# Gated unit ahead of the attention, late gates and key projections between the read-outs, mixing in each attention step, output projection by sequences

## The chip, the cores and the metric

The kernel runs on one core of one Trainium2 chip. The metric is the device time of one execution in microseconds. Five engines work side by side, each through its own list of instructions in order: TensorE (PE; its weight loads are listed apart as PEld), VectorE (DVE), ScalarE (ACT), GpSimd (POOL) and SyncE (SP). Most transfers are issued from SP's list, some from ACT's and POOL's, and an engine goes on once it has issued one.

## The reference, cut to what matters

One encoder layer is applied to two sequences of 512 tokens, width 1024, all in float32:

```python
h = rms_norm(x, ln1)
q, k, v, u, g_att, g_ssm = jnp.split(h @ w_in, IN_SPLITS, axis=-1)
q = rms_norm(q.reshape(..., 16, 64), q_gain); k = rms_norm(k.reshape(..., 4, 64), k_gain)
y_att = windowed_attention(q, k, v, sink, bias, band_mask(seq_len))
y = gelu(s5(u))
y_ssm = y * sigmoid(y @ w_glu + b_glu)
mixed = sigmoid(g_att) * y_att + sigmoid(g_ssm) * y_ssm
x = x + mixed @ w_out
h2 = rms_norm(x, ln2)
return x + square(relu(h2 @ w_up)) @ w_down
```

`s5` is a state-space recurrence in both directions over 64 groups of 16 channels. The attention has 16 heads in 4 groups (j), a band of 128 to each side and blocks of 128 queries.

## The kernel before, in words

Every large product is made in three passes (`mm3`, L164 to L166): each operand is split into a rounded part (hi, cast on ACT) and a rest (lo, subtracted on DVE), and PE adds hi·hi, lo·hi and hi·lo in one bank. So every weight that comes in passes ACT and then DVE before PE can use it.

The stages, by the times of the profile:

- 0 to 228: norm of the input, the columns of u, tables for the recurrence.
- 212 to 394: sixteen gate columns (`gate_column`; L187 evacuates, L188 writes to `ga_scr` and `gs_scr`), while DVE runs the recurrence over 64 chunks (233 to 348).
- 394 to 480: four row tiles of keys, then the states are read out. One q stands for two groups: `st` is copied from the states (L477, L479, L480), PE multiplies it with the tables `toep` (L484) and `ctab` (L487) that SP loads (L464, L466, L471), ACT applies gelu (L489), and each eight groups go out in one write from ACT's queue (L493).
- 480 to 538: the other keys in turn with four query tiles, then the values.
- 538 to 775: the attention, eight steps (j, sequence) of four units. PE, ACT and DVE follow an order written out by hand here; POOL and SP are ordered by a scheduler. A unit makes the scores of one query block, and in between projects one query tile for the next step: its norm runs over POOL (L623, L624: power; L629: copy `qn`) before PE turns it (L634). `Divide` takes the sums of a finished step, turns them, writes them out and reads them back spread over the partitions (`fac`, L724 to L730), and POOL multiplies the step's result with them (L735), which goes to `mix_scr` (L736). During step 7 the state branch's y, turned in memory by eight copies, is read back and split (L901, L902).
- 775 to 893: the gated unit, for sequence 1 and then 0, eight columns each: weights (L138, L139), gates and attention's result loaded, sigmoids (L918, L919), products on POOL (L922, L923), PE, sigmoid (L926), product and sum (L927, L928), split (L929, L930).
- 893 to 1000: output projection, row tile by row tile (both sequences' tile t in turn), each followed by norm and turning (L980, L985).
- 1000 to 1629: the MLP's two products by a scheme of seven block products; the change doesn't touch them.

Each engine's instructions outside the part ordered by hand stand in the order that the scheduler gave them. A pool's buffers decide when a load may start: it waits until the last reader of the buffer is done.

## Time and profile before

| | us |
|---|---|
| three runs | 1626.48, 1618.11, 1625.65 |
| median | 1625.65 |
| profiled execution, span | 1629.0 |
| PE busy | 1522.8 (93%) |
| DVE busy | 1140.7 (70%) |
| ACT busy | 794.0 (49%) |
| POOL busy | 172.7 (11%) |
| mean granted clock of PE | 0.977 |

The span is the time from the first to the last instruction of one execution. Matmuls overlap, so the sum of their busy time says less than the distance from start to start. A wait in the list of waits is put down to what came last.

### The profile page before, as it was taken

What the parts mean: (1) busy time and instruction counts of PE and PEld (TensorE: products, weight loads), DVE (VectorE), ACT (ScalarE), POOL (GpSimd) and SP (SyncE); (2) the same over time, 40 slices, a digit from 0 to 9 for tenths busy, and PEclk for the clock granted to TensorE, in tenths of its full rate; (3) what the DMA queues carried; (4) which work ended last, traced back from release to release, by engine and by line L of the source; (5) the groups of instructions that cost most, each with busy time, mean ns of one, the idle gap of its engine ahead of it and who ended that gap; (6) DMA issues with size and microseconds to landing.
All of it is one profiled execution on the core that took longest, in us unless ns stands there. A gap on an engine that the chain in (4) does not pass through costs nothing.

```text
span 1629.0 us, 22424 instructions
## 1 busy us (share of the span) xinstructions
PE 1522.8 (93%) x8202; PEld 1293.8 (79%) x8202; DVE 1140.7 (70%) x2006; ACT 794.0 (49%) x1398; POOL 172.7 (11%) x246
## 2 busy tenths in 40 slices
PE   4999999999779999998688997999999999999999
PEld 3778878888669988995467997888888878888787
DVE  7899969961434788889778546777777659666544
ACT  5667751222332678779555323445545434433332
POOL 2000001000013123332452000000000000000000
PEclk9999999999879999999899998999999999999999
DMA  4444458233863132213575422544444397445331
GB/s 158 131 147 142 144 172 279 98 110 111 278 211 107 33 96 76 84 55 105 199 237 171 154 84 95 168 143 142 149 149 158 131 351 258 143 145 177 124 122 65
DMA packets 115226, 240.24 MB, mean 147 GB/s; under 512 B 15355, under 2 KB 38011, under 8 KB 115116
## 3 DMA queue, kind: packets, MB, share of 16 engines
q1 hardware_dynamic: 93100, 191.47, 36.6%
q10 hardware_dynamic: 19456, 37.87, 6.1%
q0 software_dynamic: 2560, 9.48, 1.7%
q8 instruction: 64, 1.05, 0.3%
q14 instruction: 46, 0.38, 0.1%
HBM read 169.53 MB, written 81.82 MB: 154 GB/s over the span
## 4 chain that ended last, share of the span: by engine, by line
PE 72%; DVE 8%; DMA 7%; issue 6%; ACT 4%; POOL 2%; SPq 0%; ACTq 0%; POOLq 0%; DVEq 0%
PE bank L165 12%; PE bank L166 12%; PE bank L164 12%; PE acc L165 7%; PE acc L166 7%; PE acc L164 7%; PE acc L611 4%; DMA ctab_in<-ct_scr 3%; PE sps L389 2%; PE sps L409 2%; PE sps L487 2%; PE po L696 1%; DMA k<-in_w_down_dram 1%; PE sps L664 1%; PE tps L680 1%
## 5 line engine op out<-in xcount | busy, mean ns | idle before, releaser
L165 PE MATMUL bank<-b_lo,a_hi 128*128 128x512 f32 x448 | 175.2, 391 | 3.3 <-DVE b_lo L1125 3.3
L166 PE MATMUL bank<-b_hi,a_lo 128*128 128x512 f32 x448 | 175.0, 391 | 0.0
L164 PE MATMUL bank<-b_hi,a_hi 128*128 128x512 f32 x448 | 174.2, 391 | 0.0
L164 PE MATMUL acc<-hT,c_hi 128*128 128x512 f32 x384 | 152.6, 397 | 0.0
L165 PE MATMUL acc<-hT,c_hi 128*128 128x512 f32 x384 | 152.5, 397 | 0.0
L166 PE MATMUL acc<-hT,c_lo 128*128 128x512 f32 x384 | 151.1, 393 | 0.0
L164 PE MATMUL bank<-act,u_hi 128*128 128x512 f32 x376 | 147.6, 393 | 3.3 <-ACT u_hi L1022 3.3
L1124 ACT CAST a_hi<-d_a 128x1024 fp32r<-128x1024 f32 x56 | 59.0, 1054 | 182.3 <-PE bank L165 178.4
L165 PE MATMUL bank<-act,u_hi 128*128 128x512 f32 x376 | 147.5, 392 | 0.0
L166 PE MATMUL bank<-act,u_lo 128*128 128x512 f32 x376 | 146.9, 391 | 0.0
L1125 DVE TENSOR_TENSOR a_lo<-d_a,a_hi 128x1024 fp32r<-128x1024 f32 x56 | 68.5, 1223 | 99.7 <-ACT a_hi L1124 97.7
L611 PE MATMUL acc<-w_hi,hT 128*128 128x256 f32 x512 | 116.1, 295 | 0.0
L165 PEld LDWEIGHTS bank<-b_lo,a_hi 128*128 128x128 f32 x448 | 84.5, 189 | 22.1 <-DVE b_lo L1125 4.4
L166 PEld LDWEIGHTS bank<-b_hi,a_lo 128*128 128x128 f32 x448 | 84.4, 188 | 17.6
L164 PEld LDWEIGHTS bank<-b_hi,a_hi 128*128 128x128 f32 x448 | 84.5, 189 | 17.5
L139 DVE TENSOR_TENSOR c_lo<-c_raw,c_hi 128x512 fp32r<-128x512 f32 x80 | 60.9, 765 | 43.1 <-ACT c_hi L138 42.9
L611 PEld LDWEIGHTS acc<-w_hi,hT 128*128 128x128 f32 x512 | 87.0, 189 | 3.8
L138 ACT CAST c_hi<-c_raw 128x512 fp32r<-128x512 f32 x80 | 49.1, 618 | 83.5 <-PE acc L165 47.5
L164 PEld LDWEIGHTS bank<-act,u_hi 128*128 128x128 f32 x376 | 71.2, 189 | 18.7 <-ACT u_hi L1022 3.7
L164 PEld LDWEIGHTS acc<-hT,c_hi 128*128 128x128 f32 x384 | 72.7, 189 | 15.6 <-issue 1.5
L165 PEld LDWEIGHTS acc<-hT,c_hi 128*128 128x128 f32 x384 | 72.7, 189 | 15.2 <-issue 1.1
L166 PEld LDWEIGHTS acc<-hT,c_lo 128*128 128x128 f32 x384 | 72.5, 189 | 14.8 <-issue 0.2
(292 smaller groups left out, 3899.8 us busy)
## 6 DMA issues: line engine op xcount, KB each, us to landing
d_a<-a_scr SPq DMA_DIRECT2D x56, 512.0 KB
u_raw<-in_w_up_dram SPq DMA_DIRECT2D x32, 512.0 KB
a_scr<-t ACTq DMA_DIRECT2D x64, 256.0 KB
k<-in_w_down_dram SPq DMA_DIRECT2D x32, 512.0 KB
c_raw<-in_w_ug_dram SPq DMA_DIRECT2D x48, 256.0 KB
a_scr<-a ACTq DMA_DIRECT2D x48, 256.0 KB
ct_scr<-ctab SPq DMA_DIRECT2D x16, 576.0 KB
ctab_in<-ct_scr SPq DMA_DIRECT2D x16, 576.0 KB
```

Of the source, the lines that this page charges most:

```text
L138: S.copy(hi[:, sl, :], raw)
L139: sub(lo[:, sl, :], raw, hi[:, sl, :].bitcast(F32))
L164: PE.matmul(ps, a[0], b[0], start=first, stop=False)
L165: PE.matmul(ps, a[0], b[1], start=False, stop=False)
L166: PE.matmul(ps, a[1], b[0], start=False, stop=last)
L389: PE.matmul(ps[0:48, g * 144:(g + 1) * 144], lbt[:, ri, q * SG + gp * SH + g, :], ctab[:, gp * SH + g, ri].rearrange("p n c -> p (n c)"), ...
L409: PE.matmul(ps[:, i * P:(i + 1) * P], bm[:, ri, g, :], u_sb[:, gp * SH + g, :], start=True, stop=True)
L487: PE.matmul(o, ctab[:, g0 % SI + g, ri, 0:T * CH], st[:, ri, g].rearrange("p s k -> p (s k)"), start=False, stop=ri == 1)
L611: PE.matmul(self.ps, hT[sq][act][:, k, col:col + P], w[:, k % 4, :], start=i == 0, stop=i == 3 * KT - 1)
L664: PE.matmul(ps[:, 0:self.nk], qs, kk[:, self.k0 * P:self.k1 * P], start=i == 0, stop=i == 1)
L1124: S.copy(hi, src)
L1125: V.tensor_sub(lo, src, hi.bitcast(F32))
```

## The change

The change moves whole stages.

- Gates: `Gate` loads, multiplies and evacuates in pieces. Thirteen columns are made whole as before; the last three (`LATE`) and all eight row tiles of keys become a list `work` that is dealt out between the 32 read-outs. The gate of the attention gets its sigmoid at the evacuation, and that of the state branch is written in the order of y.
- Read-out: PE, ACT and DVE follow an order by hand. Tables come per two q (four groups). Each two q's result leaves in eight writes of 16 partitions from SP (L587), in the order in which y is read back later, so the eight copies in memory are gone.
- Values and y: during the eight row tiles of values y is read and split.
- The gated unit stands ahead of the attention; each column's weights are loaded once for both sequences, and the result, with its gate, goes to `z_scr`.
- Entry: the four query tiles of the first step follow one another.
- Attention: `Divide.multiply` multiplies with the factor (L903) and with the attention's gate (L905) and adds z (L906), on POOL. In step 7 the mixed rows of steps 0 to 5 are read back and split (L921 to L924); those of steps 6 and 7 are split from their buffers (`parts`, L915, L916).
- Output projection: sequence 0 by blocks of 256 columns, its rows kept in `x1p`, then sequence 1 by row tiles.

In the code `V` is DVE, `S` ACT, `GP` POOL, `SP` SyncE.

```diff
+LATE = 3
...
-    y_scr = dram.tile([T, CH, GROUPS, NSEQ * NCHUNK], F32, name="y_scr")
-    y2_scr = dram.tile([GROUPS, CH, T, NSEQ * NCHUNK], F32, name="y2_scr")
+    y_scr = dram.tile([GROUPS, CH, T, NSEQ * NCHUNK], F32, name="y_scr")
...
+    class Gate:
...
+        def evacuate(self, s):
+            if s == 0:
+                self.sg = evp.tile([P, NTOK], F32, tag="ev", name="sg")
+            if self.kind == "ga":
+                S.activation(self.sg[:, s * HALF:(s + 1) * HALF], self.ps[s], AF.Sigmoid)
+            else:
+                S.copy(self.sg.rearrange("p (t s k) -> p t s k", t=T, s=NSEQ)[:, :, s, :],
+                       self.ps[s].rearrange("p (k t) -> p t k", t=T))
+            if s == 1:
+                SP.dma_start((ga_scr if self.kind == "ga" else gs_scr)[self.c], self.sg)
...
-        gates = [(scr, base, c) for scr, base in ((ga_scr, GA_BLK), (gs_scr, GS_BLK)) for c in range(KT)]
-        for i, (scr, base, c) in enumerate(gates[:10]):
-            gate_column(c, scr, base)
+        gates = [Gate(c, kind) for kind in ("ga", "gs") for c in range(KT)]
+        for i, gate in enumerate(gates[:-LATE]):
+            gate.whole()
...
-                if (g0 + SH) % SB == 0:
-                    ga = g0 + SH - SB
-                    S.dma_start(y_scr[:, :, ga:ga + SB].rearrange("t c g k -> (t c) (g k)"),
-                                ysb.rearrange("p g k -> p (g k)"))
-            for scr, base, c in gates[10:]:
-                gate_column(c, scr, base)
...
+        def tables_in(q):
+            if q % 2:
+                return
+            g0 = q * SH
+            u_sb = sp.tile([P, SI, NSEQ * NCHUNK], F32, tag="u_sb", name="u_sb")
+            SP.dma_start(u_sb, u_scr[:, :, g0:g0 + SI].rearrange("t c g k -> (t c) g k"))
+            toep = sp.tile([P, SI, T * CH], F32, tag="toep", name="toep")
+            SP.dma_start(toep, toep_scr[:, :, g0:g0 + SI].rearrange("t c g n -> (t c) g n"))
+            ctab = sp.tile([P, SI, 2, 9 * CH], F32, tag="ctab", name="ctab_in")
+            SP.dma_start(ctab.rearrange("p g r n -> p (g r n)"),
+                         ct_scr[:, g0:g0 + SI].rearrange("p g r n -> p (g r n)"))
+            loaded[q] = loaded[q + 1] = u_sb, toep, ctab
...
+        def gelu(q):
+            if q % 2 == 0:
+                outs["y"] = sp.tile([P, SI, NSEQ * NCHUNK], F32, tag="ysb", name="ysb")
+            ysb = outs["y"]
+            S.activation(ysb[:, q % 2 * SH:(q % 2 + 1) * SH, :].rearrange("p g k -> p (g k)"),
+                         outs.pop(q)[:, 0:SH * P], AF.Gelu_apprx_tanh)
+            if q % 2:
+                g0 = (q - 1) * SH
+                for t in range(T):
+                    SP.dma_start(y_scr[g0:g0 + SI, :, t, :].rearrange("g c k -> c g k"), ysb[t * CH:(t + 1) * CH])
...
+        work = []
+        late = gates[-LATE:]
+        for n, gate in enumerate(late):
+            for s in range(NSEQ):
+                for i in range(3):
+                    work.append((lambda gate=gate: gate.multiply(8),
+                                 (lambda gate=gate, s=s: gate.evacuate(s)) if i == 2 else None))
...
+        for t in range(NT):
+            for i in range(2):
+                work.append((lambda t=t, i=i: key_mm(t, i * 12, i * 12 + 12),
+                             (lambda t=t: key_end(t)) if i == 1 else None))
+        casts = {1: [lambda: late[1].load(0), lambda: late[1].load(1)], 3: [lambda: w_k.piece(0)], 4: [lambda: w_k.piece(1)],
+                 7: [lambda: late[2].load(0), lambda: late[2].load(1)], 13: [lambda: w_k.piece(2)], 14: [lambda: w_k.piece(3)],
+                 20: [lambda: w_v.piece(0)], 21: [lambda: w_v.piece(1)], 23: [lambda: w_v.piece(2)], 24: [lambda: w_v.piece(3)]}
...
+            for q in range(NQ):
+                if q + 1 < NQ:
+                    tables_in(q + 1)
+                    turn_states(q + 1)
+                read_out(q)
+                ready, owed_k[:] = owed_k[:], []
+                subs = [cast() for cast in casts.get(q, [])]
+                for fn in ready:
+                    nxt = fn()
+                    if callable(nxt):
+                        owed_k.append(nxt)
+                until = (q + 1) * len(work) // NQ
+                for mm, end in work[done:until]:
+                    mm()
+                    if end:
+                        end()
+                done = until
+                for sub in subs:
+                    sub()
+                gelu(q)
...
+        def y_parts(m):
+            yr = y_in(m)
+            for s in range(NSEQ):
+                hi, lo = [q[:, m, :].rearrange("p (t k) -> p t k", t=T) for q in yT[s]]
+                S.copy(hi, yr[:, :, s, :])
+                V.tensor_sub(lo, yr[:, :, s, :], hi.bitcast(F32))
...
+        for t in range(NT):
+            ps = acc()[:, 0:CB]
+            w_v.multiply(ps, hT[t // 4], t % 4 * P, 0, 3 * KT)
+            y_parts(t)
+            values(t, ps)()
...
+        def gated(gs_, yr):
+            S.activation(gs_, gs_, AF.Sigmoid)
+            V.tensor_mul(gs_, gs_, yr)
+        nxt = glu_column(0)
+        for m in range(KT):
+            w, gs_, yr = nxt
+            z = gpool.tile([P, NSEQ, NCHUNK, T], F32, tag="z", name="z", bufs=1)
+            for s in range(NSEQ):
+                ps = proj_T(w, 0, yT[s])
+                if s == 0:
+                    gated(gs_, yr)
+                    if m + 1 < KT:
+                        nxt = glu_column(m + 1)
+                    else:
+                        for i in range(2):
+                            w_q0.piece(i)()
+                elif m == KT - 2:
+                    pass
+                gl = gpool.tile([P, T, NCHUNK], F32, tag="gl", name="gl")
+                S.activation(gl.rearrange("p t k -> p (t k)"), ps, AF.Sigmoid, bias=bglu_sb[:, m:m + 1])
+                V.tensor_mul(z[:, s].rearrange("p k t -> p t k"), gl, gs_[:, :, s, :])
+            SP.dma_start(z_scr[m], z.rearrange("p s k t -> p (s k t)"))
...
+                self.fac = evp.tile([P, 2, HALF], F32, tag="ev", name="fac")
...
+            def gate_in(self, scr):
+                j, sq = self.j, self.sq
+                t_ = evp.tile([P, 2, HALF], F32, tag="ev", name="gt")
+                self.queue.dma_start(t_, scr[2 * j:2 * j + 2, :, sq * HALF:(sq + 1) * HALF].rearrange("m p t -> p m t"))
+                return t_
             def multiply(self):
                 j, sq = self.j, self.sq
+                ga = self.gate_in(ga_scr)
                 GP.tensor_tensor(self.ya, self.ya, self.fac, op=ALU.mult)
-                self.queue.dma_start(mix_scr[2 * j:2 * j + 2, :, sq * HALF:(sq + 1) * HALF].rearrange("m p t -> p m t"),
-                                     self.ya)
-        column = cpool, ("c_hi", "c_lo")
-        w_k = load_qkv(w_qkv[K_BLK], [column, column])
-        for t in range(4):
-            rows_block(w_k, t, k_evac)
-        for piece in weight_pieces(0):
-            piece()()
-        load_biases(0)
-        kd = key_copies(0, 0)
-        rows = None
-        for t in range(4):
-            new = Tile(0, 0, t)
-            new.project(3 * KT)
-            new.square()
-            new.power()
-            new.norm()
-            if rows:
-                rows.turn()
-                rows.high()
-                rows.low()
-            rows = new
-            rows_block(w_k, 4 + t, k_evac)
-            if t == 0:
-                key_turn(0, 0, kd)
-        w_v = load_qkv(w_qkv[V_BLK], [(evp, ("ev", "ev")), column])
-        for t in range(NT):
-            rows_block(w_v, t, v_evac)
+                z = self.gate_in(z_scr)
+                GP.tensor_tensor(self.ya, self.ya, ga, op=ALU.mult)
+                GP.tensor_tensor(self.ya, self.ya, z, op=ALU.add)
+                if j < N_KV - 1:
+                    self.queue.dma_start(mix_scr[2 * j:2 * j + 2, :, sq * HALF:(sq + 1) * HALF].rearrange("m p t -> p m t"),
+                                         self.ya)
+            def parts(self):
+                j, sq = self.j, self.sq
+                for m in range(2):
+                    hi, lo = [q[:, 2 * j + m, :] for q in mixT[sq]]
+                    S.copy(hi, self.ya[:, m])
+                    V.tensor_sub(lo, self.ya[:, m], hi.bitcast(F32))
...
+        def mix_parts(m, sq):
+            raw = cpool.tile([P, HALF], F32, tag="c_raw", name="m_raw")
+            SP.dma_start(raw, mix_scr[m, :, sq * HALF:(sq + 1) * HALF])
+            hi, lo = [q[:, m, :] for q in mixT[sq]]
+            S.copy(hi, raw)
+            V.tensor_sub(lo, raw, hi.bitcast(F32))
...
-                    if 1 <= i < 3:
-                        t = (i - 1) * NB + qb
-                        SP.dma_start(y2_scr[:, :, t, :].rearrange("g c k -> c g k"), y_scr[t])
...
+                        made = div
+                    if i == len(steps) - 1:
+                        for n in range(qb * 3, qb * 3 + 3):
+                            mix_parts(n % 6, n // 6)
+                        if qb == NB - 1:
+                            made.parts()
...
-        for m in range(KT):
-            yr = (ap if m % 2 else evp).tile([P, T, NSEQ, NCHUNK], F32, tag="c_lo" if m % 2 else "ev", name="yr")
-            SP.dma_start(yr.rearrange("p t s k -> p (t s k)"),
-                         y2_scr[m * 8:(m + 1) * 8].rearrange("g c t k -> (g c) (t k)"))
-            for sy in range(NSEQ):
-                yv = yr[:, :, sy, :].rearrange("p t k -> p k t")
-                hi = yT[sy][0][:, m, :].rearrange("p (k t) -> p k t", t=T)
-                S.copy(hi, yv)
-                V.tensor_sub(yT[sy][1][:, m, :].rearrange("p (k t) -> p k t", t=T), yv, hi.bitcast(F32))
...
+        div.parts()
...
-        for s in (1, 0):
-            mt = mixT[s] = slot(slot_c if s == 1 else slot_a)
-            for m in range(KT):
-                w = load_column(w_glu[m], V.tensor_sub)
-                ab_ = [gpool.tile([P, HALF], F32, tag=f"mx{i}", name=f"mx{i}", bufs=4) for i in range(3)]
-                for t_, scr in zip(ab_, (mix_scr, ga_scr, gs_scr)):
-                    SP.dma_start(t_, scr[m, :, s * HALF:(s + 1) * HALF])
-                at, ga, gs_ = ab_
-                S.activation(ga, ga, AF.Sigmoid)
-                S.activation(gs_, gs_, AF.Sigmoid)
-                yy = gpool.tile([P, HALF], F32, tag="yy", name="yy")
-                V.tensor_add(yy, yT[s][0][:, m, :].bitcast(F32), yT[s][1][:, m, :].bitcast(F32))
-                GP.tensor_tensor(gs_, gs_, yy, op=ALU.mult)
-                GP.tensor_tensor(at, at, ga, op=ALU.mult)
-                ps = proj_T(w, 0, yT[s])
-                gl = gpool.tile([P, HALF], F32, tag="gl", name="gl")
-                S.activation(gl, ps, AF.Sigmoid, bias=bglu_sb[:, m:m + 1])
-                V.tensor_mul(gl, gl, gs_)
-                V.tensor_add(gl, gl, at)
-                S.copy(mt[0][:, m, :], gl)
-                V.tensor_sub(mt[1][:, m, :], gl, mt[0][:, m, :].bitcast(F32))
...
+        load_block(0)
+        for t in range(NT // 2):
+            load_rows(x10[t], t * P)
         ln2_bc = rn2.tile([P, D], F32, name="ln2_bc", bufs=1)
         SP.dma_start(ln2_bc, ln2.to_broadcast([P, D]))
-        w4 = [load_block(w_out[blk], wpool if blk < 2 else wb) for blk in range(4)]
+        for blk in range(4):
+            if blk:
+                load_block(blk)
+            for t in range(NT // 2):
+                cs = slice(t * P, (t + 1) * P)
+                ps = acc()[:, 0:CB]
+                proj_rows(ps, w4[blk], mixT[0], t * P)
+                xs = x10[t][:, blk * CB:(blk + 1) * CB]
+                V.tensor_add(xs, ps, xs)
+                if blk == 3:
+                    for dst, src_ in zip((B11, B21), norm_rows(x10[t], t * P)):
...
-                for b in range(2):
-                    ps = acc()
-                    for e in range(2):
-                        proj_rows(ps[:, e * CB:(e + 1) * CB], w4[b * 2 + e], mixT[sq], t * P)
...
+                    proj_rows(ps[:, e * CB:(e + 1) * CB], w4[b * 2 + e], mixT[1], t * P)
...
```

SP's queue in the read-out before: the tables alone (the write of y is ACT's).

```order
L466 DMA toep<-toep_scr 128x1024
L471 DMA ctab_in<-ct_scr 128x1152
L464 DMA u_sb<-u_scr 128x1024
L471 DMA ctab_in<-ct_scr 128x1152
L466 DMA toep<-toep_scr 128x1024
```

And now, from the last whole gate on, where `w_raw` are the keys' weights:

```order
L205 DMA gs_scr<-sg 128x1024
L546 DMA toep<-toep_scr 128x512 x2
L544 DMA u_sb<-u_scr 128x512
L546 DMA toep<-toep_scr 128x512
L587 DMA y_scr<-ysb 16x4x128 x8
L548 DMA ctab_in<-ct_scr 128x1152
L508 DMA w_raw<-in_w_qkv_dram 128x512 x2
L544 DMA u_sb<-u_scr 128x512
L546 DMA toep<-toep_scr 128x512
L548 DMA ctab_in<-ct_scr 128x1152
L587 DMA y_scr<-ysb 16x4x128 x8
```

Eight small writes now stand among the table loads of SP for each two q, and the first table's load behind the last whole gate's write.

POOL in an attention step before, around the product with the factor (`ms`, `rq`, `qn` belong to the query tile of the next step):

```order
L735 TENSOR_TENSOR ya<-ya,fac 128x1024
L623 TENSOR_SCALAR ms<-ms 128x4
L624 TENSOR_TENSOR rq<-ms,neg_half 128x4
L629 COPY qn<-qn 128x4x64
L656 COPY p<-nsink 128x4
```

And now:

```order
L903 TENSOR_TENSOR ya<-ya,fac 128x1024
L905 TENSOR_TENSOR ya<-ya,gt 128x1024
L785 TENSOR_SCALAR ms<-ms 128x4
L786 TENSOR_TENSOR rq<-ms,neg_half 128x4
L906 TENSOR_TENSOR ya<-ya,gt 128x1024
L791 COPY qn<-qn 128x4x64
```

Two operations on 128x1024 have come in, one ahead of the tile's power and one between power and copy.

ACT at the end of the attention now; `act` are the mixed rows' parts, `w_0` is the first block of the output weights:

```order
L846 CAST ph<-tps 128x512
L886 COPY row<-tps 16x128
L862 COPY ol<-po 64x512
L923 CAST act_8620<-m_raw 128x512
L915 CAST act_8618<-ya 128x512 x2
L915 CAST act_8620<-ya 128x512 x2
L1105 CAST w_0_9004<-w_raw 128x512 x4
```

The casts of the output weights stand behind the parts of the last divide's rows; before, the gated unit's weights (L138) followed the parts of y.

397 lines of the change are left out of this document (237 added, 160 removed).

## The prediction

> **What bounds the kernel now.** I read the page first, then the busy times by windows, then TensorE's (PE) waits, then single stretches of the timeline. From the page, the span, PE's own row and its forty slices:
>
> ```profile
> span 1629.0 us, 22424 instructions
> PE 1522.8 (93%) x8202; PEld 1293.8 (79%) x8202; DVE 1140.7 (70%) x2006; ACT 794.0 (49%) x1398; POOL 172.7 (11%) x246
> PE   4999999999779999998688997999999999999999
> PEclk9999999999879999999899998999999999999999
> ```
>
> PE is the bound nearly everywhere, and the change leaves its number of matmuls alone. So all that can change is how long PE stands still, and that is worst in two dips: slices 11 to 12 and 19 to 22 (of 40.7 us each), with a small one in 25. Busy time of PE, PEld, DVE, ACT, POOL, then granted clock, DMA share and GB/s, by windows of 60 us:
>
> ```profile
> 420.00:480.00 60.00, 43.03 (x272) 40.02 (x271) 23.11 (x32) 18.12 (x33) 0.41 (x3) 0.83 0.74 249
> 600.00:660.00 60.00, 58.18 (x427) 53.37 (x428) 50.83 (x132) 46.55 (x116) 20.84 (x37) 1.00 0.25 76
> 720.00:780.00 60.00, 50.21 (x281) 38.38 (x280) 55.59 (x126) 52.51 (x114) 14.95 (x22) 0.97 0.31 99
> 780.00:840.00 60.00, 45.14 (x182) 34.72 (x181) 42.63 (x48) 30.30 (x49) 29.86 (x21) 0.89 0.65 214
> 840.00:900.00 60.00, 52.60 (x236) 41.41 (x235) 46.69 (x59) 32.98 (x56) 21.61 (x14) 0.97 0.58 188
> 960.00:1020.00 60.00, 51.60 (x352) 47.90 (x351) 33.59 (x50) 18.11 (x32) 3.15 (x8) 0.91 0.27 93
> ```
>
> The attention (538 to 740) is nearly full; the read-out of the states (420 to 480) and the gated unit with the step before it (720 to 900) are not. What PE waited for between 393 and 1013:
>
> ```profile
> PE sps L487 <- DMA ctab_in<-ct_scr: 16.1, 7, 3.7
> PE acc L164 <- ACT c_hi L138: 14.2, 4, 11.5
> PE acc L634 <- POOL qn L629: 5.7, 16, 2.2
> PE sps L985 <- DVE rn_xn L980: 5.5, 2, 4.6
> PE bank L164 <- ACT u_hi L1022: 3.3, 1, 3.3
> ```
>
> The table loads of the read-out, the weights of the gated unit, and small waits for POOL in the attention.
>
> **How I count.** Durations of pipelined matmuls overlap, so I count from start to start. Rows of the timeline: half a read-out (6 records), two 256-column matmuls, two 512-column ones:
>
> ```profile
> 475.42 0.39 PE L484 MATMUL sps<-u_sb,toep 128*128 128x128 f32 x2
> 476.09 0.39 PE L484 MATMUL sps<-u_sb,toep 128*128 128x128 f32 x2
> 618.79 0.28 PE L664 MATMUL sps<-kh,qa 128*128 128x256 f32 x1
> 618.90 0.28 PE L664 MATMUL sps<-kl,qa 128*128 128x256 f32 x1
> 789.74 0.39 PE L165 MATMUL acc<-act,c_hi 128*128 128x512 f32 x1
> 789.97 0.39 PE L166 MATMUL acc<-act,c_lo 128*128 128x512 f32 x1
> ```
>
> One q of the read-out is 1.34 us (2 x 0.67), a 256-column matmul 0.12, a 512-column one 0.227. First and last starts, from the listing by source line, give the stages:
>
> ```profile
> L187 ACT COPY sg<-acc x32: 570/580/588, 212.3 to 393.8; 128x512 f32<-128x512 f32 x32
> L664 PE MATMUL sps<-kh,qa x128: 274/335/687, 538.0 to 766.8; 128*128 128x256 f32 x64, 128*128 128x384 f32 x64
> L696 PE MATMUL po<-pl,va x80: 387/397/766, 547.4 to 774.9; 128*128 128x512 f32 x80
> L928 DVE TENSOR_TENSOR gl<-gl,mx x16: 676/684/1789, 801.3 to 895.0; 128x512 f32<-128x512 f32 x16
> ```
>
> **1. Read-out and projections of keys and values.** Before: from the last gate (393.5) to the first scores (538.0) are 144.5 us. Work: 32 q x 1.34 = 42.9; keys 192, values 192 and four query tiles 96 matmuls of 256 columns, 480 x 0.12 = 57.6; turns 2: together 102.5. PE lost 42. In the change three gates (3 x 48 x 0.227 = 32.6) and the keys' rows stand between the read-outs, so one pair of q has 6.2 us of work, and the tables have time to come. Against that stand three costs.
>
> Start: the first table's load is behind the last whole gate's write on SP, and no key rows stand in between now: evacuation 0.58, two issues, landing, 5 us of idle.
>
> Steady state: each pair's result now leaves SP in 8 small writes of 32 KB, before on ACT's queue in one per four q; most often they stand ahead of the tables for the pair after next. The nearest rows: an issue of the same kind of scatter (L328), and a table load from issue to use (the second of the pair's issues ends at 473.41, PE goes on at 477.47):
>
> ```profile
> L328 SPq DMA_DIRECT2D u_scr<-up x64: 570/570/722, 53.2 to 198.3; - x64
> 466.19 7.22 SPq L471 DMA_DIRECT2D ctab_in<-ct_scr  x2
> 469.00 1.19 PE L487 MATMUL sps<-st,ctab_in 128*128 128x128 f32 x4 [1.88 <-DMA ctab_in<-ct_scr]
> ...
> 470.41 1.91 PE L487 MATMUL sps<-st,ctab_in 128*128 128x128 f32 x8
> ...
> 474.53 1.06 PE L487 MATMUL sps<-st,ctab_in 128*128 128x128 f32 x8
> ...
> 477.47 0.68 PE L487 MATMUL sps<-st,ctab_in 128*128 128x128 f32 x4 [0.98 <-DMA ctab_in<-ct_scr]
> ```
>
> From the last read-out of a pair: gelu 0.4 to 2.4 (it stands behind the casts), 8 issues 2.6 (at 0.32, a plain issue) to 4.9 (at 0.57 + 0.04), three table issues 1.0, landing 2.8 to 5: 6.8 to 13.3 us. The slack is the other half's work and the next pair, 1.7 + 6.2 = 7.9. Late by nothing to 5.4 us in each of 8 double pairs: 0 to 43. I take gelu 1.4, issues 3.8, landing 4: 10.2, late by 2.3, 18.5 us.
>
> By the Trainium skill, page "DMA: Bandwidth & Descriptors", section Bandwidth, transfers under 64 KB are dominated by their descriptors; that speaks against 32 KB writes and would put this at the upper end, 43 us. The trace has no such write on SP beside table loads, so it decides neither.
>
> Values and the entry with its four query tiles, now without key rows between: 3 us each (0 to 6: the first part of y can be read only after the last write, some 9 us after the last read-out, against one row of values, 2.9, in each of three accumulators). Sum after: 5 + 18.5 + 6 = 29.5, a gain of 12.5 (from 12 lost to 31 gained).
>
> **2. The gated unit and the last step.** Before, from step 7 (538.0 + 7 x 28.8 = 739.6) to 893.5: 154 us. Work: 16 x 24 x 0.227 = 87.1, and of step 7 28.75 less four query tiles (24 x 0.12 + 0.5 each) = 15.2. Lost: 51.5, among them the 11.5 wait for c_hi. After: the unit runs ahead of the attention with its input there and each weight loaded once: 2. Step 7 keeps its units' length, since ACT and DVE set it (the window 600 to 660 has both at about 80%, and three parts of 0.62 and 0.69 take the query tile's place): 28.75 - 15.2 = 13.5.
>
> Then the last divide. Before, it ran beside the gated unit. After, the casts of the output weights stand on ACT and DVE behind the parts of the last mixed rows, which wait for POOL. Both projections' weights are therefore late, and so is sequence 0, which needs nothing of that divide. How long the divide takes, from the last value matmul (774.9):
>
> ```profile
> 778.28 1.21 POOL L730 DMA_DIRECT2D fac<-rs_scr  x2 [1.66 <-DMA rs_scr<-row]
> 783.58 2.40 POOL L735 TENSOR_TENSOR ya<-ya,fac 128x1024 f32<-128x1024 f32 x1 [4.09 <-DMA fac<-rs_scr]
> L138 ACT CAST c_hi<-c_raw x80: 600/621/634, 24.8 to 887.4; 128x512 fp32r<-128x512 f32 x80
> ```
>
> 785.98 is 11.1 after it; gate multiplication 2.4, wait for z (its slot is free only after the first product, landing as fac: 4.1) 1.7 beyond that, addition 2.4, two parts and a cast 1.9, a subtraction 0.7: 20. Bounds: 8 (if the weights' casts got in front) and 24. Sum after 2 + 13.5 + 20 = 35.5, a gain of 16.
>
> **3. POOL in the attention.** Each step has on POOL, between the factor and the query tile, not one product of 2.4 us but product, product and sum; the order is product, product, power, sum, qn. Step 2's unit before:
>
> ```profile
> 618.24 2.39 POOL L735 TENSOR_TENSOR ya<-ya,fac 128x1024 f32<-128x1024 f32 x1 [1.69 <-DMA fac<-rs_scr]
> 620.71 0.23 POOL L623 TENSOR_SCALAR ms<-ms 128x4 f32<-128x4 f32 x1
> 621.02 1.04 POOL L624 TENSOR_TENSOR rq<-ms,neg_half 128x4 f32<-128x4 f32 x1
> 622.58 0.40 POOL L629 COPY qn<-qn 128x256 f32<-128x256 f32 x1 [0.52 <-DVE qn L628]
> 623.03 0.66 PE L634 MATMUL acc<-ident,qn 128*128 128x128 f32 x4 [0.36 <-POOL qn L629]
> 646.41 2.40 POOL L735 TENSOR_TENSOR ya<-ya,fac 128x1024 f32<-128x1024 f32 x1 [0.38 <-DMA fac<-rs_scr]
> ```
>
> PE already waits 0.36 for qn, so there is no slack. After: products end at 623.05, power at 624.4, sum at 626.8, qn at 627.2 in place of 622.98: 4.2 us. Six steps (1 to 6; step 7 has no query tile): 25. Bounds: 12 (the sum falls behind qn) and 36 (z, loaded only after the first product, comes 2 us later). The wait of 2.2 at the attention's start goes. Net loss 23.
>
> **4. Output projection by sequences.** Same matmuls. Sequence 0's rows are normalized while sequence 1 is multiplied, so the first products of the up projection wait for one row tile's tail, not for four blocks': of the 8.8 us of L980 and L1022 I expect 5 gained (-3 to 9).
>
> **5. Clock after waits.** After the 1.88 us wait above the next four records took 1.19 us, where others take 0.61, and the eight after them were slow too, about 1.4 us in all; the window 420 to 480 was granted 0.83. Three long new waits (start, divide, end of the projection) at 1.4: 4 lost. Whether the six waits of 4.2 in the attention cost clock as well is rival D.
>
> **Sum:** -12.5 - 16 + 23 - 5 + 4 = -6.5. The profiled 1629.0 becomes 1622.5; the median of the three runs stands 0.2% lower than the span, so 1625.65 becomes about 1619. It is a large gain in two dips given back to POOL.
>
> **The rivals.**
>
> A (forecast, 0.43): as above, 1619, own range 1605 to 1632.
>
> B (0.20): POOL and the divide don't bite: the factor comes earlier or the sum lies behind qn without delaying it, and the loss of 25 falls to 5; and the last divide costs 8. 1619 - 20 - 12 = 1587. For it: POOL is busy 20.84 of 60 in the attention window, so there is room. Against it: the order is fixed and PE's slack there is none.
>
> C (0.25), slower: SP becomes the clock of the read-out. Its 8 small writes wait each for the DMA eight before it, beside loads at 249 GB/s, so that a pair takes 8.7 us instead of 6.2: 16 x 2.5 = 40 instead of 18.5, 1641; at 9.1 a pair 1648. It decides from about 0.8 us per write (8 x 0.8 + 1.0 for the tables + gelu 1.3). For it: L328's 0.57 with nothing else under way, and the page's rule on small transfers. Against it: 0.8 is not seen in any row.
>
> D (0.12): PE's clock falls after each wait for POOL as it did in the read-out: 6 x 1.4 = 8 more, 1627, no change. For it: the row of 1.19 above. Against it: nothing but that the wait of 2.2 at the attention's start is the only one of its kind there. By the Trainium skill, page "TensorE: Matmul & The Clock Gate", Part 1, an idle window of about 3.4 us halves the clock for as long again; by that rule an estimate would be 1.7 for each wait, 10 in all.
>
> **How the numbers follow.** About 0.5% (8 us) is what can be told from no change. A (0.43) lies round that bound: 0.21 faster, 0.15 same, 0.07 slower. B 0.20 faster. C 0.23 slower, 0.02 same. D 0.02 faster, 0.07 same, 0.03 slower. Together faster 0.43, same 0.24, slower 0.33. The range for 8 in 10 leaves out the ends of B and C, a tenth each: 1585 to 1648.
>
> **What would show it.** In the changed kernel's waits and windows, right: waits of PE for qn of about 4 us, once in each of six steps; one wait of about 20 after the last value matmul, ending on the cast of the output weights; PE busy over 50 of 60 us in the read-out; hardly a wait in the gated unit. Wrong: qn waits under 1 us (3); output matmuls within 10 us of the last value matmul (2); a stage from the last whole gate to the first value row over 140 us (1, rival C), or under 105.

## The result, and the profile after

The changed kernel takes 1694.03 us (median of four runs, 1693.76 to 1702.9), the kernel before beside it on the same chip 1626.07: a ratio of 1.0445, 95% interval 1.0406 to 1.0485. It is slower by 4.4%, where 1619 was forecast and 1648 was the range's end. The profiled execution spans 1691.9, 62.9 more than before.

The page's first parts of the changed kernel (span, busy time, PE's forty slices, the granted clock):

```profile
span 1691.9 us, 22497 instructions
PE 1528.2 (90%) x8202; PEld 1306.4 (77%) x8202; DVE 1106.9 (65%) x1978; ACT 767.6 (45%) x1359; POOL 163.3 (10%) x231
PE   5899999987788999888974599799999999999999
PEclk9999999998889999999997799799999999999999
```

PE has the same 8202 records, so the difference is standing still and a lower clock. Before, there were two dips; now there is a longer one (slices 9 to 12), a shallow one through the attention (17 to 19) and a deep one (slices 22 and 23). The windows that answer to those of before (busy time of PE, PEld, DVE, ACT, POOL, then granted clock, DMA share, GB/s):

```profile
360.00:420.00 60.00, 46.29 (x256) 40.22 (x256) 17.19 (x24) 17.89 (x32) 0.00 (x0) 0.88 0.57 171
420.00:480.00 60.00, 46.59 (x292) 42.54 (x291) 18.40 (x28) 14.23 (x28) 4.75 (x6) 0.86 0.60 177
540.00:600.00 60.00, 60.00 (x261) 49.51 (x261) 25.35 (x28) 19.10 (x29) 0.00 (x0) 0.98 0.58 199
720.00:780.00 60.00, 51.51 (x358) 47.16 (x357) 42.94 (x113) 38.96 (x98) 28.10 (x36) 0.94 0.33 99
840.00:900.00 60.00, 41.41 (x269) 36.89 (x267) 37.69 (x99) 35.92 (x90) 19.70 (x27) 0.89 0.25 78
900.00:960.00 60.00, 24.92 (x117) 21.22 (x118) 24.89 (x50) 18.94 (x42) 14.68 (x10) 0.65 0.42 126
1020.00:1080.00 60.00, 46.90 (x340) 44.33 (x340) 43.52 (x65) 19.07 (x33) 3.16 (x8) 0.90 0.25 88
```

The gated unit (540 to 600) is full; the read-out (360 to 480) is still poor and lasts longer; the attention (720 to 780) has lost its full clock (0.94). What PE waited for between 340 and 1090:

```profile
PE acc L796 <- POOL qn L791: 24.5, 21, 3.9
PE sps L826 <- DVE nmx L830: 24.5, 5, 10.7
PE acc L153 <- ACT w L1105: 22.6, 2, 22.4
PE sps L574 <- DMA ctab_in<-ct_scr: 13.3, 6, 3.1
PE tps L1125 <- DVE rn_xn L1119: 12.3, 6, 8.8
PE sps L572 <- DMA toep<-toep_scr: 9.9, 4, 3.2
```

Rows three and one were forecast (last divide, POOL's order). Row two (step 7) and row five (output projection) were not, and the waits for tables in the read-out, which should have shrunk, grew (13.3 and 9.9, where 16.1 was before).

Counted from start to start over every matmul of both traces (what lies beyond the usual distance of its shape is lost):

| stretch of PE's work | before, lost us | after, lost us |
|---|---|---|
| up to the first read-out | 38.5 | 42.9 |
| read-out | 40.4 | 46.1 |
| rest of the keys, values, query entry | 3.8 | 8.7 |
| gated unit | 32.5 | 2.5 |
| attention, steps 0 to 6 | 15.5 | 45.5 |
| step 7 | 16.7 | 36.0 |
| last value matmul to output projection | 0 | 22.6 |
| output projection | 16.5 | 26.9 |
| MLP | 10.3 | 7.0 |
| sum | 174.2 | 238.2 |

The work is 1436.8 us in both. The gated unit's 30 us were won as intended. They are given back in the attention (30), and twice over in step 7 and behind it.

### The profile page after: what moved, and what is told of

The parts are those of the page before. It is cut to its first block, busy times and chain, and to the rows that moved or that the text cites. A ratio compares the mean times of both kernels' runs of the same rounds, so it can differ in the third digit from the quotient of the medians.

```text
span 1691.9 us, 22497 instructions
## 1 busy us (share of the span) xinstructions
PE 1528.2 (90%) x8202; PEld 1306.4 (77%) x8202; DVE 1106.9 (65%) x1978; ACT 767.6 (45%) x1359; POOL 163.3 (10%) x231
## 4 chain that ended last, share of the span: by engine, by line
PE 69%; DMA 10%; issue 6%; DVE 6%; POOL 4%; ACT 3%; SPq 2%; ACTq 0%; POOLq 0%; DVEq 0%
PE bank L154 12%; PE bank L155 12%; PE bank L153 12%; PE acc L192 9%; PE acc L515 4%; PE acc L154 3%; PE acc L155 3%; PE acc L153 3%; PE sps L415 2%; PE sps L435 2%; DMA w_raw<-in_w_out_dram 2%; DMA ctab_in<-ct_scr 2%; DMA gt<-z_scr 1%; DMA fac<-rs_scr 1%; PE sps L574 1%
## 5 line engine op out<-in xcount | busy, mean ns | idle before, releaser
L515 PE MATMUL acc<-w_hi,hT 128*128 128x256 f32 x768 | 173.8, 303 | 3.2 <-DVE va L680 2.6
L192 PE MATMUL acc<-hT,c_hi 128*128 128x512 f32 x512 | 165.5, 402 | 0.0
L515 PEld LDWEIGHTS acc<-w_hi,hT 128*128 128x128 f32 x768 | 134.9, 200 | 8.2 <-DVE va L680 2.8
L192 PEld LDWEIGHTS acc<-hT,c_hi 128*128 128x128 f32 x512 | 98.0, 193 | 20.9 <-issue 1.3
L515 PE MATMUL acc<-w_lo,hT 128*128 128x256 f32 x384 | 112.0, 292 | 0.8 <-DVE w_lo L510 0.8
L192 PE MATMUL acc<-hT,c_lo 128*128 128x512 f32 x256 | 102.2, 399 | 0.0
L153 PEld LDWEIGHTS bank<-b_hi,a_hi 128*128 128x128 f32 x448 | 84.1, 188 | 17.5
L153 PE MATMUL acc<-w,act 128*128 128x256 f32 x256 | 73.0, 289 | 22.6 <-ACT w L1105 22.6
L836 ACT ACTIVATE p<-p,nmx 128x257 f32<-128x257 f32 (+1 forms) x128 | 72.3, 565 | 31.6 <-DVE nmx L830 30.8
L153 PEld LDWEIGHTS bank<-act,u_hi 128*128 128x128 f32 x376 | 71.2, 189 | 19.4 <-ACT u_hi L1205 4.5
L155 PEld LDWEIGHTS bank<-act,u_lo 128*128 128x128 f32 x376 | 71.3, 190 | 15.0
L154 PEld LDWEIGHTS bank<-act,u_hi 128*128 128x128 f32 x376 | 71.3, 190 | 14.7
```

Of the source, the lines that this page charges most:

```text
L153: PE.matmul(ps, a[0], b[0], start=first, stop=False)
L154: PE.matmul(ps, a[0], b[1], start=False, stop=False)
L155: PE.matmul(ps, a[1], b[0], start=False, stop=last)
L192: PE.matmul(self.ps[s], self.w[p == 2][:, k, :], hT[s][p == 1][:, k, :], start=i % (3 * KT) == 0, stop=i % (3 * KT) == 3 * KT - 1)
L515: PE.matmul(ps, act[p == 2][:, k, col:col + P], self.w[k // 4][p == 1][:, k % 4, :], start=i == 0, stop=i == 3 * KT - 1)
L836: S.activation(p, p, AF.Exp, bias=self.nmx[:, h:h + 1], scale=-1.0, accum_out=self.sums[:, h, self.qb:self.qb + 1])
```

## The experiments

All are made from the changed kernel, one edit each until the last three. Spans are of one profiled execution, to be held against 1691.9. The four executions of the changed kernel spanned 1691.4 to 1700.5, so a gain under 10 is read only beside the loss of the stage that it comes from, counted from start to start as in the table.

**Read-out: the tables ahead of the small writes.**

```diff
-                    tables_in(q + 1)
...
+                if q % 2 and q + 3 < NQ:
+                    tables_in(q + 3)
                 gelu(q)
```

> The tables of the pair after next are issued on SP ahead of the eight small writes of the pair just read out, no other edit. Theory (the tables come late because they stand behind those writes): the read-out, 140 us from first to last matmul, falls to 110 to 118, the waits for toep and ctab from 23 to under 8 us, the span from 1692 to 1663 to 1670. Rival (the queue's transfers themselves are slow, 171 GB/s with many 512-byte packets): under 8 us gained, the waits for tables stay above 16.

1691.7: nothing gained, and the read-out takes 135.5 instead of 140.2. PE's waits in the read-out of this kernel (to be held against 13.3 and 9.9 for the tables above):

```profile
PE sps L572 <- ACT ysb L582: 13.1, 5, 5.2
PE sps L572 <- issue: 4.4, 1, 4.4
...
PE sps L574 <- DMA ctab_in<-ct_scr: 3.5, 3, 2.1
```

The waits for tables fell from 23 to 3.5 us as the theory had it, but the span did as the rival had it, for PE now waits 13.1 for gelus. SP (first two rows) and ACT ahead of one of these waits, which ends at 428.32:

```profile
418.14 5.31 SPq L587 DMA_DIRECT2D y_scr<-ysb  x8
423.55 0.37 SPq L508 DMA_DIRECT2D w_raw<-in_w_qkv_dram  x1
```

```profile
427.37 0.62 ACT L509 CAST w_hi<-w_raw 128x512 fp32r<-128x512 f32 x1 [9.92 <-DMA w_raw<-in_w_qkv_dram]
427.89 0.38 ACT L582 ACTIVATE ysb<-sps 128x256 f32<-128x256 f32 x1
```

The key weights' load stands behind the eight writes on SP. The cast that waits for it stands ahead of the gelu on ACT, and PE needs the bank that the gelu empties. All five waits for gelus end right behind such a cast. So SP issues three kinds of transfer here: tables, weights and small writes. With the tables first, the weights are still late. It is so in the changed kernel too, with one more turn: the late gelu makes the writes late, and the tables behind them.

```profile
400.57 1.28 ACT L184 CAST c_hi<-c_raw 128x512 fp32r<-128x512 f32 x2 [10.71 <-DMA c_raw<-in_w_ug_dram]
```

Behind this cast the gelu of one pair came 10.2 us after the pair's last read-out. ACT's casts waited 39.6 us for weights in the read-out of the changed kernel, 56.3 with the tables first.

**Read-out: one write for eight, and other queues for the eight.**

```diff
-                for t in range(T):
-                    SP.dma_start(y_scr[g0:g0 + SI, :, t, :].rearrange("g c k -> c g k"), ysb[t * CH:(t + 1) * CH])
+                SP.dma_start(y_scr[g0:g0 + SI].rearrange("g c t k -> (c t) g k"), ysb)
```

> Each pair's result leaves in one write with the same 512-byte runs in place of eight; the order on SP stays. The rows of y land in other places, so the output is not the reference's. Theory (issue time of eight writes ahead of the tables): 3.6 to 5.5 us become 0.4, the read-out falls by 20 to 28 us. Rival (a late gelu behind casts that wait for their weights holds the write and with it the tables): under 10 us gained, and the gaps stay at the pairs with a cast.

The two others keep the loop, with `GP.dma_start` and `S.dma_start` in the place of `SP.dma_start`.

> The 128 small writes of y are issued from POOL's queue instead of SP's; same sizes, same places. Theory (SP's in-order queue is the clock of the read-out: three tables, eight writes and their waits take 8.7 us of a pair's 6.2): the read-out falls from 140 to 99 to 108 us, span 1650 to 1660. Rival (small transfers hold the DMA engines or their in-flight places, whoever issues them): the read-out stays above 125.

> The same writes from ACT's queue, whose DMAs, like SP's, each wait for the hardware DMA eight before. Theory (SP's queue alone): as with POOL's queue, 99 to 108 us, if ACT's own time (eight issues of 0.45, 3.6 us of a pair's 6.2) leaves room. Rival (the eight places in flight, shared by both queues): above 125, and ACT's waits move into the gelus and casts.

First and last start of the read-out's first matmul of a group (L572), for the changed kernel, one write, POOL's queue, ACT's queue, in this order:

```profile
L572 PE MATMUL sps<-u_sb,toep x128: 270/275/553, 364.5 to 504.2; 128*128 128x128 f32 x128
```

```profile
L572 PE MATMUL sps<-u_sb,toep x128: 270/275/426, 364.5 to 463.3; 128*128 128x128 f32 x128
```

```profile
L572 PE MATMUL sps<-u_sb,toep x128: 270/275/422, 365.0 to 471.1; 128*128 128x128 f32 x128
```

```profile
L572 PE MATMUL sps<-u_sb,toep x128: 270/275/581, 364.3 to 486.5; 128*128 128x128 f32 x128
```

139.7, 98.8, 106.1 and 122.2 us; the spans are 1691.9, 1642.5, 1658.7 and 1670.0. 98.8 is the 98.5 of pure work (32 x 1.34 + 32.6 + 192 x 0.12). One write carries the same 512-byte runs as eight, so neither the bytes nor their runs cost the 41 us; the number of transfers that one in-order queue has to issue does. With one write the casts wait 0.5 us for weights up to the end of the read-out, so their lateness was a part of the loop and not its start, and the rival of the late gelu falls. On POOL's queue, idle there, nearly the same is won with all the small writes, so their size costs 7 at most. On ACT's queue, between what the theory and the rival had said, the wait moves again, since ACT's own work stands behind the writes. ACT's timeline in that kernel:

```profile
405.07 3.93 ACTq L587 DMA_DIRECT2D y_scr<-ysb  x8
409.11 0.38 ACT L582 ACTIVATE ysb<-sps 128x256 f32<-128x256 f32 x1 [4.06 <-DMA y_scr<-ysb]
...
412.15 6.03 ACTq L587 DMA_DIRECT2D y_scr<-ysb  x8
418.30 0.38 ACT L582 ACTIVATE ysb<-sps 128x256 f32<-128x256 f32 x1 [6.18 <-DMA y_scr<-ysb]
```

The gelus of the next pair wait 4 to 6 us for eight issues. The rival of shared places in flight (SP's and ACT's transfers take eight semaphores in turn here, so each waits for the one eight before it) isn't ruled out for ACT's case: eight issues there took up to 6.03, 0.75 each.

**Attention: POOL's order.** POOL joins the order by hand, and the three operations are called one unit apart (what the scheduler did with them before is the order in the section on the change).

```diff
+                    if i > 0 and qb == 2:
+                        made.multiply()
+                    if i > 0 and qb == 3 and nxt:
+                        made.gate()
...
+                    if qb == 0:
+                        if i > 1:
+                            made.plus()
```

> POOL's order in the attention is written out: product with the factor behind the copy qn of the third unit, product with the gate behind that of the fourth, sum behind that of the next step's first. The same work on POOL. Theory (the six waits of 3.2 to 4.1 us come from POOL's order alone): they vanish, 20 to 24 us gained, 1668 to 1672. Rival (POOL's work slows DVE's operations on SBUF, and z comes late): the waits move to other places, under 8 gained.

1661.3, 30.6 less. POOL in the changed kernel, at the product of a step's third unit, and PE behind it:

```profile
690.81 2.39 POOL L903 TENSOR_TENSOR ya<-ya,fac 128x1024 f32<-128x1024 f32 x1 [0.37 <-DMA fac<-rs_scr]
693.28 2.39 POOL L905 TENSOR_TENSOR ya<-ya,gt 128x1024 f32<-128x1024 f32 x1
695.75 0.23 POOL L785 TENSOR_SCALAR ms<-ms 128x4 f32<-128x4 f32 x1
696.07 1.04 POOL L786 TENSOR_TENSOR rq<-ms,neg_half 128x4 f32<-128x4 f32 x1
697.31 2.35 POOL L906 TENSOR_TENSOR ya<-ya,gt 128x1024 f32<-128x1024 f32 x1 [0.21 <-DMA gt<-z_scr]
699.60 0.40 POOL L791 COPY qn<-qn 128x256 f32<-128x256 f32 x1
```

```profile
700.05 1.11 PE L796 MATMUL acc<-ident,qn 128*128 128x128 f32 x4 [3.49 <-POOL qn L791]
700.96 1.06 PE L842 MATMUL tps<-ident,p 128*128 128x128 f32 x4
701.67 0.56 PE L515 MATMUL acc<-w_hi,hT 128*128 128x256 f32 x1
...
706.54 0.60 PE L842 MATMUL tps<-ident,p 128*128 128x128 f32 x4
```

And with POOL's order by hand, the same wait, and the whole of steps 0 to 6 in one window:

```profile
PE acc L796 <- POOL qn L791: 4.5, 15, 0.4
```

```profile
641.00:844.00 203.00, 196.70 (x1442) 180.10 (x1441) 173.90 (x454) 160.60 (x399) 95.61 (x135) 1.00 0.29 87
```

POOL does the same work, and PE doesn't wait for it over 0.4 us any more. The steps are 203 us instead of 232, as long as the 202 of the kernel before. Only the order was wrong. The gain of the steps, 29, is more than the six waits (3.0 to 3.9, together 20.9): behind the wait above PE runs slow, four turns in 1.06 us instead of 0.60, and the changed kernel's window from 720 to 780, shown above, is granted 0.94 where this kernel has 1.00 over all seven steps.

**Step 7: buffers of their own for the rows read back.**

```diff
-            raw = cpool.tile([P, HALF], F32, tag="c_raw", name="m_raw")
-            SP.dma_start(raw, mix_scr[m, :, sq * HALF:(sq + 1) * HALF])
+            raw = m_raws[m // 2, sq][:, m % 2]
```

> The mixed rows that step 7 reads back get buffers of their own (those of weights no longer used), six loads issued at the end of step 6, in place of twelve through two buffers. Theory (step 7 stands still because DVE and ACT, in order, wait for these loads and hold the scores' maxima): the three gaps of 7, 10.9 and 6.3 us go, 16 to 24 gained, 1668 to 1676. Rival (the parts' work itself is too much for DVE): under 6 gained.

1676.9, 15 less. In the changed kernel SP (first two rows), ACT, DVE and PE around the longest wait:

```profile
894.38 0.87 SPq L921 DMA_DIRECT2D m_raw<-mix_scr  x2
899.60 0.37 SPq L897 DMA_DIRECT2D gt<-z_scr  x1
```

```profile
899.24 0.62 ACT L923 CAST act<-m_raw 128x512 fp32r<-128x512 f32 x1 [5.63 <-DMA m_raw<-mix_scr]
```

```profile
899.89 2.64 DVE L924 TENSOR_TENSOR act<-m_raw,act 128x512 fp32r<-128x512 f32 x1 [5.48 <-ACT act L923]
902.46 0.60 DVE L830 CUSTOM_DVE_ANT_0 p<-sps,bias,nsink 128x384 f32<-128x384 f32 x1
```

```profile
903.12 0.69 PE L826 MATMUL sps<-kh,qa 128*128 128x384 f32 x1 [10.74 <-DVE nmx L830]
```

Two buffers mean that the third load of a unit starts when the first part is done; its landing holds ACT, ACT holds DVE, DVE can't take the next unit's maxima, and PE stands 10.7 us. About 2 us of these are another thing: the subtraction L924 takes 2.64 here and 0.69 elsewhere. Beside it POOL runs the product with the gate (L905, 899.65 to 901.99). The theory's size was a little high: the wait for maxima fell from 24.5 to 12.0, not to nothing. That the rest is the three parts, which still stand ahead of the maxima, is likely but not shown. Of the 15, step 7 gives 10. The rest comes from elsewhere: SP has no reads to issue just before the last divide's write, and the divide's transfers are faster (from the write of the sums to the product 7.4 us instead of 12.7), so the wait for the output weights falls from 22.6 to 17.0.

**The last divide taken out of the way.**

```diff
-        div.multiply()
         div.parts()
+        div.multiply()
```

> The parts of the last step are made from the rows before the factor, the gate and z are applied (those are left out of the output of that step), so nothing of the output projection waits for POOL. Theory (PE's 22.8 us after the last value matmul are the last divide's chain): 3 to 6 us remain, 1672 to 1676. Rival (the output weights themselves come late, issued only 1.6 us before that matmul): above 12 remain.

1682.6, 9 less, where 16 to 20 were expected. PE's wait behind the last value matmul is 4.2 instead of 22.6, as the theory said. But ACT then meets this:

```profile
930.91 0.62 ACT L1105 CAST w<-w_raw 128x512 fp32r<-128x512 f32 x1 [0.27 <-DMA w_raw<-in_w_out_dram]
939.13 1.27 ACT L1105 CAST w<-w_raw 128x512 fp32r<-128x512 f32 x2 [7.60 <-DMA w_raw<-in_w_out_dram]
```

The output weights come through two buffers, and the second half of the first block is 7.6 us late. So the output projection loses 10.9 more than in the changed kernel (31.7 against 20.8 up to its last turn). Theory and rival hold, one behind the other: the divide's chain hides the late weights.

**Output projection: a temporary of its own.**

```diff
-            tx = rn2.tile([P, 2, 4, P], F32, tag="xn", name="tx", bufs=1)
-            tt = [tx[:, 0], tx[:, 1]]
+            tt = [wb.tile([P, 4, P], F32, tag="w_raw", name="tx", bufs=2) for _ in range(2)]
```

> In the output projection's second half the temporary of the sums (tx) gets buffers of its own instead of the one it shares with the normalized row (rn_xn). Theory (a row tile's chain of square, power, norm, turn and nine operations, 14 us one after the other through that buffer, is longer than its 11.5 us of matmuls): the 8.8 us wait at the last tile shrinks to under 4, 5 to 9 gained. Rival (DVE's own time): under 2.

1684.8, 7 less. The wait for the normalized row in this kernel (12.3, longest 8.8, in the changed one):

```profile
PE tps L1125 <- DVE rn_xn L1119: 7.4, 4, 5.7
```

In the changed kernel the square of the next row tile (1048.85, 1062.20) begins only when the temporary's last reader is done, every 13.35 us, against 11.5 of matmuls (96 x 0.12). With its own buffer it goes ahead, and the output projection loses 6.5 less up to its last turn. The gain is as the theory said, but the longest wait is 5.7, not under 4: square, power, norm and turn of the last tile remain.

**Together.**

> Four edits together: small writes from POOL's queue, POOL's order written out, own buffers for the rows read back, own temporary in the output projection. If each removes a loss of its own the gains add: 33 + 30 + 15 + 7 = 85 below the changed kernel's 1692, 1604 to 1612. Rival (they share a loss, the later stages' waits return when the earlier ones go): above 1625.

1600.9 (one timed run 1602.71, the kernel before beside it 1621.86). The sum of the four single gains (33.2 + 30.6 + 15.0 + 7.1 = 85.9) gives 1606.0, 5 more than measured, so the losses were separate as far as single executions can tell.

> The same, and in step 7 one part at a time between the unit's other work instead of three at its end, and in the last divide the gate's product ahead of the factor, with gate and z loaded beforehand. Theory (PE's 17 us after the last value matmul are POOL's chain behind the factor; step 7's waits for the maxima are the three parts ahead of them on DVE): 4 to 5 less after the last value matmul, 3 to 8 less in step 7, 1592 to 1604, faster than both kernels. Rival (step 7 is set by ACT and DVE's total work): step 7 keeps its length.

1606.76 us (median of four, 1605.23 to 1610.61), ratio to before 0.9913 (0.9893 to 0.9932), span 1604.4: faster than both, but not than the four alone. The last divide went nearly as expected (from the last value matmul to the output projection 12.4 us instead of 16.1). Step 7 became longer, against theory and rival: from its last query turn to the last value matmul 41.4 us instead of 34.9. Parts between a unit's operations hold DVE's low halves (`pl`), PE's next values wait for them in 7 places:

```profile
PE po L858 <- DVE pl L851: 11.5, 7, 2.6
```

> The four edits and the last divide's gate product ahead of the factor, with step 7's parts at its units' ends again. If the interleaved parts alone made the run before slower and the last divide's 3.7 us hold: 1596 to 1602 and step 7 at 38 us. Rival (the longer step 7 had another cause): 1604 to 1608.

1601.09 us (median of four, 1598.67 to 1604.95), ratio to before 0.9866, interval 0.9843 to 0.9889; span 1598.8. 11.6 us remain behind the last value matmul. Step 7 is shorter again (38.8 us), as expected, but still 3.9 longer than with the four. One wait for maxima is 6.2 where it was 3.0, behind three subtractions that take 5.51 us in this kernel (first row) and 2.30 with the four (last row), though nothing in them was changed:

```profile
834.11 5.51 DVE L946 TENSOR_TENSOR act<-m_raw,act 128x512 fp32r<-128x512 f32 x3 [1.73 <-ACT act L945]
836.13 2.34 POOL L919 TENSOR_TENSOR ya<-ya,gt 128x1024 f32<-128x1024 f32 x1 [0.43 <-DMA gt<-z_scr]
```

```profile
834.31 2.30 DVE L938 TENSOR_TENSOR act<-m_raw,act 128x512 fp32r<-128x512 f32 x3 [1.72 <-ACT act L937]
```

Two of POOL's operations (L915 from 833.35, then the L919 shown) run beside them in this kernel; with the four, they meet for under 1 us in all. So against the four alone (1600.9) the two together are worth nothing that can be told.

```profile
span 1598.8 us, 22530 instructions
...
PE   4999999998999999999965997999999999999999
```

The change with its five repairs is 1.3% faster than the kernel before. What is left is one dip (slices 21 and 22): step 7 and the last divide.

## Why the prediction was wrong, point by point

The sum was made of -12.5 (read-out, keys, values), -16 (gated unit, step 7, last divide), +23 (POOL), -5 (output projection), +4 (clock). Measured from the table: +15, +12, +30, +7 (with the MLP's -3), the clock being in them. From the forecast -6.5 to the table's 64 it is 70 us: 28 in the second term (step 7), 27 in the first (read-out), 12 in the output projection, 7 in POOL's, less the 4 that had been set aside for the clock. The read-out's queue and the clock behind POOL's waits were seen and set too low; step 7's loads and the output projection's buffer were not seen.

*1, the read-out: the step that failed is the chain's middle value, "late by 2.3".* The chain from the last read-out of a pair to its table was put at 10.2 us against a slack of 7.9. The stage's 140.2 us are 17.5 for two pairs where 12.4 are work: late by 5.1, near the upper bound of 5.4 and not the middle. The link that was too short is the gelu, put at 0.4 to 2.4 behind the casts: the casts were costed and not their wait for weights, whose loads stand on the same queue, and in five of 16 pairs the gelu came 4.4 to 10.2 us after the last read-out. Eight issues took 3.6 to 5.5, not far from the 2.6 to 4.9 said. The start's 5 us were right (the row of 4.4 above). Rival C had the stage's time right, 8.7 a pair against 140.2/16 = 8.76, and that was luck: it asked for 0.8 a write, where 3 of 128 took that and the median issue was 0.43. SP isn't full (its issues are 77 us of the 140). Being in order, it is late with whichever kind of transfer stands behind the small writes (the first experiment), and one queue for all is the cause (the one write and POOL's queue). The Trainium skill, page "DMA: Bandwidth & Descriptors", section Bandwidth, speaks against transfers under 64 KB. I let that rule decide nothing, and it pointed the right way, though the loss isn't in the transfers themselves: 120 writes of 32 KB cost 41 us over 15 of 256 KB on SP's queue, and the same 120 cost 7 on POOL's.

*2, the gated unit: right* (2.5 lost, 2 said). *Step 7: the step that failed is "step 7 keeps its units' length".* It was costed by the busy time of ACT and DVE, with three parts of 0.62 and 0.69 in the place of a query tile, and without the loads that feed them: 36 lost instead of 13.5. Two buffers make these loads a chain through SP, ACT and DVE; the own buffers show it, for 10 of the 36. Step 7 still loses 26 then, twice what was said, so the place of the parts ahead of the maxima was too cheap as well; how much of it is that, and how much POOL's products beside DVE's subtractions, stays open.

*The last divide: right,* 22.6 where 20 was said, and for the reason said (4.2 remain without it). What was not seen is that the output weights behind it are late too.

*3, POOL: right in place and nearly in size,* waits of 3.0 to 3.9 in each of six steps (4.2 said), 20.9 us where 25 was said. Rival B (POOL doesn't bite) is refuted: it bites, and by its order alone. Rival D is right as an addition: of the 29 us by which the steps grew, 8 are not in the waits, and the granted clock is 0.96 over the steps where it is 1.00 with POOL's order by hand. Behind the wait of 3.49 it is half for 6.8 us, behind four of the others for 3.4, and behind one of 3.46 not at all. By the Trainium skill, page "TensorE: Matmul & The Clock Gate", Part 1, half speed follows an idle window of about 3.4 us. The trace agrees in the length of most slow stretches, but the length of one wait doesn't decide here, for in the read-out the clock fell to half behind a wait of 2.25 too. Against D I had only the wait of 2.2 in the kernel before, behind which the clock stayed at 1.00.

*4, the output projection: the step that failed is the sign of "5 gained".* I looked at what the up projection waits for and not at the row tiles in between. Before, the temporary was used once for two row tiles (23 us of matmuls); by sequences, it is used once for one row tile, 11.5 against a chain of 13.35.

*5, the clock: too small,* 4 for three waits. In the read-out alone the waits sum to 26.3 of the 46.1 lost (13.3, 9.9, 2.4 and 0.7). The granted clock is 0.87 over its 140 us, which makes an estimate of 18 more; with one write for eight it is 0.98.

## What to carry to other kernels

A stage moved to where PE has time takes its transfers with it: count, for each queue that issues in order, how many it must issue for one round of the loop and who waits for each kind, not the bytes; where it is too many, another engine's idle queue is worth more than another order. Before a side engine gets more work, look at where in its own order it will stand, for the same work one place later can cost nothing; a scheduler may put it at the worst place. And cost a moved operation with its load and its buffers, and a cast with the wait for its weight: with two buffers, three loads in a unit are a chain.

## What the runs showed of the hardware that was not expected

120 writes of 32 KB in place of 15 of 256 KB, with the same runs of 512 bytes and the same total, cost 41 us of the read-out on SP's queue, 7 on POOL's and 23 on ACT's. The first product of the last divide started 12.7 us after its sums were written out where SP issued five reads within 2.3 us around that write, and 7.4 where it issued none, though the divide's transfers were issued by POOL. Six waits of PE of 3.0 to 3.9 us cost about 8 us more in clock. DVE's subtractions of 128x512 took 1.4 to 2.85 us where a product of POOL ran beside them for more than a microsecond, and 0.70 at most where POOL did nothing.
